# Prompt attention, selected branch: values stationary and exponentials as two float32r parts, the other branch unchanged

## The chip, the cores and the metric

The kernel runs on one core of one Trainium2 chip. The metric is device time in microseconds (us) of one execution, the median of several. In what follows PE is TensorE, PEld its weight loads, DVE VectorE, ACT ScalarE, POOL GpSimd and SP SyncE; SP and ACT also issue transfers.

## What is computed

One inference step of a decoder of two layers, for a prompt of 2048 tokens and eight sample sequences of 8 tokens each. Layer 0 is retention beside sparse attention with three branches (compressed, selected, sliding window); layer 1 is an S5 state-space mixer with a gated output. The change touches the selected branch of the prompt's attention. The reference, cut to it:

```python
s2 = jnp.einsum('bqghd,bgqkd->bqghk', qblk, kg).astype(f32) * scale
p2 = jax.nn.softmax(jnp.where(m2, s2, NEG_INF), axis=-1)
o_sel = jnp.einsum('bqghk,bgqkd->bqghd', p2.astype(vg.dtype), vg)
...
o = gblk[..., 0:1] * o_cmp + gblk[..., 1:2] * o_sel + gblk[..., 2:3] * o_win
```

For each query and group of four heads, `kg` and `vg` are the keys and values of the 8 selected blocks of 64 tokens. The kernel computes the branch densely: every tile of 128 keys up to the query's own, with a large negative bias on blocks that aren't selected.

## The kernel before

The span has three stages: projections and retention to about 780 us; the attention with its output projection from about 816 to 2112; and the S5 layer (setup, a sweep over the tokens that projects its input, the scan, the outputs, a last sweep) to the end. Instructions are written by Python generators that are woven together, and a list scheduler then settles the order on every engine; what an engine does is thus an order fixed when the kernel is built.

**The attention** works in 32 units: unit u is the query tile t = u mod 16 (128 queries) of head group u // 16 (four heads). `first(u)` loads and splits keys and queries (`keys`, L995, `queries`, L1018) and makes the compressed scores; `second(u)` finds the row maxima (`maxima`, L1126: score matmuls L1140 into PSUM, reductions L1142 or, under a mask, L1146 on DVE), writes their negative, times constants, as four extra rows of the queries (L1161 on POOL), and sums the compressed values (`values1`, L1092 to L1102). `body(u)` runs `loop(u, 1)`, the window, then `loop(u, 0)`, the selected branch. While unit u runs its loops, `second(u + 1)`, `first(u + 2)` and a filling stream are woven in: in the first head group the sample sequences, in the second the output projection (`project`, L1299: transposes L224, matmuls L269 to L271 in three float32r parts, additions L1313).

**A loop** takes one step for each key tile k: t + 1 steps in the selected branch (272 over all units), min(t, 4) + 1 in the window (140). A step (L1164 to L1194) makes the scores of 128 keys by 4x128 queries in one PSUM tile `st` (two buffers; matmuls L1186 and L1187 with float32r operands, 512 columns each, and L1189 under a mask), takes the exponential on ACT into `pe` in SBUF (L1191, five buffers), and AVL = 2 steps later multiplies it with the values. This product (`product`, L1173 to L1175) holds the exponentials of one head, 128 keys by 128 queries, as weights and moves the 65 columns of `VP`: 64 values and a column of ones, so that the row sum comes out beside the output. The four heads have a matmul each, into one tile `ot` of PSUM (two buffers):

```python
for h in range(4):
    nc.tensor.matmul(out=ot[:, h], lhsT=pe[:, 128 * h:128 * h + 128], rhs=VP[br][:, k % nt[br]], ...)
```

All four are in float32. At the end of a loop `weighted` (L1203) is put into the list `late`, and `finish` (L1213) behind the selected one; they are written out some steps into a following loop. `weighted` takes the reciprocal of the 65th column (L1207), multiplies it with the gate (L1208), scales the output with it (L1210), all on DVE, and adds it to `o2` on POOL (L1211). `finish` multiplies by the other gate (L1217) and stores the unit's output.

**Behind the attention** come on SP the weights of the odd layer (L188, `wraw`), the sample's tiles and the S5 sweep (L1608 to L1670: normalisation on POOL or DVE, L210 and L1614; transposes L1626; matmuls L1665 to L1667). Before the sweep, or beside it, stands the setup of the S5 parameters (`discretise`: loads L1467 to L1471, a long chain of small DVE operations L1452 to L1580, round trips through memory `at_s`, L1561 to L1563) and what is computed from it in `tables_in` (L1384 to L1424).

## Time and profile before

| | |
|---|---|
| median of 3 runs | 3415.76 us (3409.8 to 3424.2) |
| the profiled execution | 3436.16 us, its span 3434.4 us |
| mean granted clock of TensorE | 0.951 of full speed |
| PE busy | 3190.7 us (93%) |
| PEld busy | 2652.5 us (77%) |
| DVE busy | 1621.4 us (47%) |
| ACT busy | 1077.6 us (31%) |
| POOL busy | 647.5 us (19%) |
| transfers | 362.83 MB, 106 GB/s over the span |

The span reaches from the first to the last instruction on the chip; the execution's own time is 1.8 us longer. Busy shares are means over the whole span; the stages have different limits, so the rows below are taken by stage. A matmul's busy time is taken from its start to its modelled end and overlaps with the next one's; what a matmul adds to the time is read from the chain, where the pieces follow one another.

### The profile page before, as it was taken

The page shows a single profiled execution, that of the slowest core. Times are in us where ns is not written, and L with a number is a line of the kernel's source. Part 1 is how long each engine was busy: PE and PEld are TensorE (multiplying, and loading weights), DVE is VectorE, ACT ScalarE, POOL GpSimd, SP SyncE. Part 2 cuts the span into 40 slices and gives each one's busy share as a digit, 9 for nine tenths or more (in the row PEclk, how much of TensorE's full clock was granted, in tenths as well). Part 3 has the DMA queues.
Part 4 walks back from the last instruction along what each step waited for, and adds up shares of the span by engine and source line. Part 5 has one row for each costly group of instructions (what it writes and reads, how often), then busy time and mean ns, then how long its engine had stood idle before and what let it go on. Part 6 is the DMA issues. An engine that isn't in the chain of part 4 may idle for free.

```text
span 3434.4 us, 47838 instructions
## 1 busy us (share of the span) xinstructions
PE 3190.7 (93%) x17745; PEld 2652.5 (77%) x17745; DVE 1621.4 (47%) x4172; ACT 1077.6 (31%) x2394; POOL 647.5 (19%) x739
## 2 busy tenths in 40 slices
PE   7999999996999999988999998799898497999999
PEld 5888878875778888867888887698676376888887
DVE  6545544444566654446555552547529603111322
ACT  4223312113444443333333332343335233111100
POOL 1211221122211111011111100232439350000000
PEclk9999999997999998878999999799999798999999
DMA  5333531204222222223211112556774286222342
GB/s 171 109 109 136 181 77 38 46 18 129 87 90 81 70 76 70 70 61 100 75 58 54 47 41 80 147 171 184 210 217 136 94 255 179 74 72 72 119 133 89
DMA packets 313680, 362.83 MB, mean 106 GB/s; under 512 B 132296, under 2 KB 225672, under 8 KB 311144
## 3 DMA queue, kind: packets, MB, share of 16 engines
q1 hardware_dynamic: 243576, 240.77, 23.9%
q10 hardware_dynamic: 63632, 73.84, 6.3%
q0 software_dynamic: 6240, 45.17, 3.7%
q8 instruction: 140, 2.29, 0.3%
q14 instruction: 92, 0.75, 0.1%
HBM read 240.50 MB, written 123.31 MB: 106 GB/s over the span
## 4 chain that ended last, share of the span: by engine, by line
PE 70%; DVE 8%; DMA 4%; ACT 1%; issue 1%; SPq 1%; POOL 1%; ACTq 0%; DVEq 0%; POOLq 0%
PE ot L1175 11%; PE mm L269 7%; PE mm L270 7%; PE mm L271 7%; PE tp L1140 4%; PE st L1186 3%; PE st L1187 3%; PE acc L269 2%; PE acc L753 2%; PE acc L271 2%; PE acc L270 2%; PE mm L1667 2%; PE mm L1665 2%; PE mm L1666 2%; DVE scan L1792 1%; PE acc L910 1%
## 5 line engine op out<-in xcount | busy, mean ns | idle before, releaser
L1175 PEld LDWEIGHTS ot<-VP,pe 128*128 128x128 f32 x3296 | 439.2, 198 | 33.1 <-issue 5.6
L1175 PE MATMUL ot<-VP,pe 128*128 128x65 f32 x3296 | 427.9, 275 | 0.0
L1191 ACT ACTIVATE pe<-st 128x512 f32<-128x512 f32 x412 | 243.6, 597 | 374.1 <-PE st L1187 293.3
L269 PE MATMUL mm<-we_hi,hT_hi 128*128 128x512 f32 x768 | 305.3, 398 | 0.2 <-ACT hT_hi L225 0.2
L270 PE MATMUL mm<-we_lo,hT_hi 128*128 128x512 f32 x768 | 303.3, 395 | 0.0
L271 PE MATMUL mm<-we_hi,hT_lo 128*128 128x512 f32 x768 | 302.4, 394 | 0.0
L269 PE MATMUL mm<-wz_hi,hT_hi 128*128 128x512 f32 x384 | 159.0, 414 | 57.8 <-ACT zr L1700 43.6
L1146 DVE CUSTOM_DVE_ANT_0 tp<-tp,tri 128x256 f32<-128x256 f32 (+3 forms) x352 | 173.7, 504 | 78.2 <-PE tp L1140 71.9
L269 PE MATMUL mm<-we,hT_hi 128*128 128x512 f32 x512 | 202.1, 395 | 6.5 <-ACT hT_hi L239 6.2
L270 PE MATMUL mm<-we,hT_hi 128*128 128x512 f32 x512 | 200.4, 391 | 0.0
L271 PE MATMUL mm<-we,hT_lo 128*128 128x512 f32 x512 | 200.3, 392 | 0.0
L1140 PE MATMUL tp<-KA,QA 96*128 96x512 f32 (+6 forms) x576 | 198.5, 394 | 0.7 <-DVE mc L1142 0.3
L1186 PE MATMUL st<-QB,KB 128*128 128x512 f32 x412 | 183.8, 448 | 2.2 <-ACT pe L1191 2.1
L1142 DVE TENSOR_REDUCE mc<-tp 128x1 f32<-128x512 f32 (+2 forms) x196 | 129.7, 671 | 93.7 <-PE tp L1140 92.8
L1187 PE MATMUL st<-QA,KA 100*128 100x512 f32 (+1 forms) x412 | 171.2, 417 | 1.1 <-POOL QA L1161 1.1
L269 PEld LDWEIGHTS mm<-we_hi,hT_hi 128*128 128x128 f32 x768 | 145.0, 189 | 30.6 <-issue 1.0
L271 PEld LDWEIGHTS mm<-we_hi,hT_lo 128*128 128x128 f32 x768 | 144.8, 189 | 30.5 <-issue 0.7
L270 PEld LDWEIGHTS mm<-we_lo,hT_hi 128*128 128x128 f32 x768 | 145.0, 189 | 29.1 <-issue 0.7
L271 PE MATMUL mm<-wz_hi,hT_lo 128*128 128x512 f32 x384 | 155.5, 405 | 5.5 <-POOL hT_lo L240 5.4
L270 PE MATMUL mm<-wz_lo,hT_hi 128*128 128x512 f32 x384 | 155.1, 404 | 0.0
L1665 PE MATMUL mm<-h_hi,wu_hi 128*128 128x256 f32 x512 | 148.9, 292 | 3.3 <-ACT uT_out L1670 3.3
L1161 POOL TENSOR_TENSOR QA<-pms,c_nd 4x512 fp32r<-4x512 f32 x64 | 66.9, 1046 | 439.0 <-ACT pms L1160 421.7
(550 smaller groups left out, 6980.9 us busy)
## 6 DMA issues: line engine op xcount, KB each, us to landing
xT_in<-xT_s SPq DMA_DIRECT2D x48, 512.0 KB
x_in<-x_prompt SPq DMA_DIRECT2D x32, 512.0 KB
xT_s<-xT ACTq DMA_DIRECT2D x32, 512.0 KB
x_in<-x_s SPq DMA_DIRECT2D x32, 512.0 KB
wraw<-w_in_even SPq DMA_DIRECT2D x24, 512.0 KB
qd<-q_s SPq DMA_DIRECT2D x64, 128.0 KB
o_in<-o_s SPq DMA_DIRECT2D x16, 512.0 KB
x_s<-x_in ACTq DMA_DIRECT2D x16, 512.0 KB
```

Of the source, the lines that this page charges most:

```text
L269: nc.tensor.matmul(out=ps[:, 0:n], lhsT=hi[:, k], rhs=whi[:, k], start=k == 0, stop=False)
L270: nc.tensor.matmul(out=ps[:, 0:n], lhsT=hi[:, k], rhs=wlo[:, k], start=False, stop=False)
L271: nc.tensor.matmul(out=ps[:, 0:n], lhsT=lo[:, k], rhs=whi[:, k], start=False, stop=k == 7)
L753: nc.tensor.matmul(out=pp[:, 0:256], lhsT=q["wc"][:, c, lp].rearrange("p r e -> p (r e)"), rhs=xt[:, j].rearrange("p g n -> p (g n)"), sta ...
L1140: nc.tensor.matmul(out=pv[:, h], lhsT=qa[0:kmask, h0 + h], rhs=KA[br][0:kmask, (k0 % nt[br]) * 128:(k0 % nt[br] + w) * 128], start=True, s ...
L1142: nc.vector.tensor_reduce(out=mc[:, h0:h0 + hw, i], in_=pv, axis=AX.X, op=OP.max)
L1146: nc.vector.tensor_tensor_reduce(out=pv[:, h], in0=pv[:, h], in1=tri[:, m0:m0 + w].rearrange("p a b -> p (a b)"), scale=1.0, scalar=-3e38, ...
L1175: nc.tensor.matmul(out=ot[:, h], lhsT=pe[:, 128 * h:128 * h + 128], rhs=VP[br][:, k % nt[br]], start=k == lo and h == 0, stop=k == u and h ...
L1186: nc.tensor.matmul(out=ps, lhsT=KB[br][:, kc], rhs=qb, start=True, stop=False)
L1187: nc.tensor.matmul(out=ps, lhsT=KA[br][0:r0 + 4, kc], rhs=qa[0:r0 + 4].rearrange("p h q -> p (h q)"), start=False, stop=k not in masked)
L1191: nc.scalar.activation(out=pe, in_=ps, func=AF.Exp, scale=0.125)
L1665: nc.tensor.matmul(out=ps[:, 0:256], lhsT=whi[:, k], rhs=hi[:, k], start=k == 0, stop=False)
```

## The change

For the selected branch alone the two operands of the product trade places. The values become the weights: `VP[0]` holds for each key tile 128 columns, 64 of the values rounded to float32r and 64 of what rounding left (hi and lo), made on POOL from a loaded tile `vr` (L1007 and L1008 of the changed kernel). The exponentials become the moving operand, also in two float32r parts: ACT writes the rounded exponential `ph` (L1215) and the full one `pe` (L1216), and DVE subtracts, `pl` = `pe` - `ph` (L1217). The product is two matmuls of 512 columns, `ph` and `pl`, summed in one PSUM tile of 128x512, whose rows are the output's 64 columns from hi and 64 from lo (L1190, L1191). There is no column of ones: POOL sums `pe` over the steps into `ac` (`add`, L1182, none for the first step of a unit). At a unit's end two copies on ACT and an addition on DVE join the halves into `OB`; `total` (in place of `weighted`) transposes the sum (L1244) and the output (L1248) on PE, four matmuls each, reduces the sum on DVE (L1246) and goes on as `weighted` did. The window branch stays as it was. Lines behind L1175 move by up to 52 in the changed kernel (L1142 becomes L1147, L1161 L1166, L1186 L1205, L1313 L1365, L1467 L1519).

```diff
@@ -949,9 +949,11 @@
         KA = [cp.tile([128, nt[i] * 128], F32R, name=f"KA{i}") for i in range(2)]
         KB = [cp.tile([128, nt[i] * 128], F32R, name=f"KB{i}") for i in range(2)]
 
-        VP = [cp.tile([128, nt[i], 65], F32, name=f"VP{i}") for i in range(2)]
-        for v in VP:
-            nc.gpsimd.memset(v[:, :, 64:65], 1.0)
+        VP = [cp.tile([128, nt[0], 2, 64], F32R, name="VP0"), cp.tile([128, nt[1], 65], F32, name="VP1")]
+        T["ac"] = P_("acb", 2)
+
+        OB = T["OB"] = [cp.tile([64, 4, 128], F32, name=f"OB{i}") for i in range(2)]
+        nc.gpsimd.memset(VP[1][:, :, 64:65], 1.0)
         nc.gpsimd.memset(KA[0][96:100].bitcast(F32), 1.0)
         nc.gpsimd.memset(KA[1][64:68].bitcast(F32), 1.0)
 
@@ -1000,7 +1002,10 @@
             for d in range(2):
                 nc.sync.dma_start(out=kd[:, 0, d], in_=self.ks_s[c, 256 + c0:320 + c0])
                 nc.sync.dma_start(out=kd[:, 1, d], in_=self.kw_s[t][:, c0:64 + c0])
-            nc.sync.dma_start(out=VP[0][:, u % nt[0], 0:64], in_=self.ks_s[c, 384 + c0:448 + c0])
+            vr = kv.tile([128, 64], F32, name="vr")
+            nc.sync.dma_start(out=vr, in_=self.ks_s[c, 384 + c0:448 + c0])
+            nc.gpsimd.tensor_copy(out=VP[0][:, u % nt[0], 0], in_=vr)
+            nc.gpsimd.tensor_tensor(out=VP[0][:, u % nt[0], 1], in0=vr, in1=VP[0][:, u % nt[0], 0], op=OP.subtract)
             nc.sync.dma_start(out=VP[1][:, u % nt[1], 0:64], in_=self.kw_s[t][:, 128 + c0:192 + c0])
             nc.sync.dma_start(out=ka[64:96], in_=a["kaux"][:, c])
             ps = tp.tile([128, 4, 128], F32, name="tp")
@@ -1166,11 +1171,25 @@
             lo, masked = span(u, br)
             r0 = 96 if br == 0 else 64
 
-            ot = T["ot"].tile([128, 4, 65], F32, name="ot")
+            ot = T["ot"].tile([128, 4, 65] if br else [128, 512], F32, name="ot", tag="ot")
+            pes, n_add = [], [0]
+
+            def add():
+
+                x, y = pes[0], pes.pop(1)
+                pes[0] = T["ac"].tile([128, 512], F32, name="ac") if n_add[0] == 0 else x
+                n_add[0] += 1
+                nc.gpsimd.tensor_tensor(out=pes[0], in0=x, in1=y, op=OP.add)
+
             qb = c["QB"].rearrange("p h q -> p (h q)")
             prods = []
 
-            def product(k, pe):
+            def product(k, pe, pl):
+                if br == 0:
+                    v = VP[0][:, k % nt[0]].rearrange("p a d -> p (a d)")
+                    nc.tensor.matmul(out=ot, lhsT=v, rhs=pe, start=k == lo, stop=False)
+                    nc.tensor.matmul(out=ot, lhsT=v, rhs=pl, start=False, stop=k == u)
+                    return
                 for h in range(4):
                     nc.tensor.matmul(out=ot[:, h], lhsT=pe[:, 128 * h:128 * h + 128], rhs=VP[br][:, k % nt[br]], start=k == lo and h == 0, stop=k == u and h == 3)
 
@@ -1188,17 +1207,50 @@
                 if k in masked:
                     nc.tensor.matmul(out=ps, lhsT=idr, rhs=triT[:, masked[k]].unsqueeze(1).to_broadcast([128, 4, 128]), start=False, stop=True)
                 pe = T["pp"].tile([128, 512], F32, name="pe")
-                nc.scalar.activation(out=pe, in_=ps, func=AF.Exp, scale=0.125)
-                prods.append((k, pe))
+                if br:
+                    nc.scalar.activation(out=pe, in_=ps, func=AF.Exp, scale=0.125)
+                    prods.append((k, pe, None))
+                else:
+                    ph, pl = [T["pp"].tile([128, 512], F32R, name=n, bufs=3) for n in ("ph", "pl")]
+                    nc.scalar.activation(out=ph, in_=ps, func=AF.Exp, scale=0.125)
+                    nc.scalar.activation(out=pe, in_=ps, func=AF.Exp, scale=0.125)
+                    nc.vector.tensor_tensor(out=pl, in0=pe, in1=ph, op=OP.subtract)
+                    pes.append(pe)
+                    if len(pes) > 1:
+                        add()
+                    prods.append((k, ph, pl))
                 if len(prods) > AVL:
                     product(*prods.pop(0))
                 yield
             for p in prods:
                 product(*p)
-            late.append((n_loop[0], lambda: weighted(u, br, ot)))
-            if br == 0:
+            if br:
+                late.append((n_loop[0], lambda: weighted(u, br, ot)))
+            else:
+                acc, ob = pes[0], T["OB"][u % 2].rearrange("p h q -> p (h q)")
+                nc.scalar.copy(out=ob, in_=ot[0:64])
+                x = TM("ox", 512)[0:64]
+                nc.scalar.copy(out=x, in_=ot[64:128])
+                nc.vector.tensor_tensor(out=ob, in0=ob, in1=x, op=OP.add)
+                late.append((n_loop[0], lambda: total(u, acc)))
                 late.append((n_loop[0], lambda: finish(u)))
             yield
+
+        def total(u, acc):
+
+            c = ctx[u]
+            ps, p = [tp.tile([128, 4, 128], F32, name="tp") for _ in range(2)]
+            for h in range(4):
+                nc.tensor.transpose(ps[:, h], acc[:, 128 * h:128 * h + 128], ident)
+            rs = sm.tile([128, 4], F32, name="rs0")
+            nc.vector.tensor_reduce(out=rs, in_=ps, axis=AX.X, op=OP.add)
+            for h in range(4):
+                nc.tensor.transpose(p[:, h, 0:64], T["OB"][u % 2][:, h], ident[0:64, 0:64])
+            nc.vector.reciprocal(out=rs, in_=rs)
+            nc.vector.tensor_tensor(out=rs, in0=rs, in1=c["gt"][:, :, 1], op=OP.mult)
+            o1 = TM("o1", 4, 64)
+            nc.vector.tensor_tensor(out=o1, in0=p[:, :, 0:64], in1=rs.unsqueeze(2).to_broadcast([128, 4, 64]), op=OP.mult)
+            nc.gpsimd.tensor_tensor(out=c["o2"], in0=c["o2"], in1=o1, op=OP.add)
 
         def weighted(u, br, ot):
 
```

The scheduler's order moves with it, at the places below (of the changed kernel numbers behind a name tell tiles apart).

On PE, in the selected loop of unit 28 (the 13th query tile of the second head group), beside the maxima of unit 29 (`tp`) and the output projection (`acc`), before:

```order
L1186 MATMUL st<-QB,KB_6636 128x512
L1187 MATMUL st<-QA,KA_6634 128x512
L1175 MATMUL ot<-VP_6638,pe 128x65 x4
L1140 MATMUL tp<-KA_6634,QA 128x384
L269 MATMUL acc<-wo_hi,hT_hi 128x512
L270 MATMUL acc<-wo_lo,hT_hi 128x512
L271 MATMUL acc<-wo_hi,hT_lo 128x512
```

and of the change:

```order
L1205 MATMUL st<-QB,KB_6636 128x512
L1206 MATMUL st<-QA,KA_6634 128x512
L271 MATMUL acc<-wo_hi,hT_lo 128x512
L1145 MATMUL tp<-KA_6634,QA 128x512
L1190 MATMUL ot<-ph,VP_6638 128x512
L1191 MATMUL ot<-pl,VP_6638 128x512
L269 MATMUL acc<-wo_hi,hT_hi 128x512
L270 MATMUL acc<-wo_lo,hT_hi 128x512
```

The four products of a step are two, behind the scores of a later step as before, with other matmuls between.

On POOL, around the selected loop of unit 15, the last of the first head group, where the keys and values of the second group are being prepared, before:

```order
L1161 TENSOR_TENSOR QA<-pms,c_nd 4x512
L1056 TENSOR_TENSOR e_13583<-e_13583,s_13666 128x4x16
L1016 CAST KA_6634<-kx 32x128 x3
L1161 TENSOR_TENSOR QA<-pms,c_nd 4x512
L1016 CAST KA_6634<-kx 32x128 x4
L1211 TENSOR_TENSOR o_13347<-o_13347,o_14022 128x256
```

and of the change:

```order
L1182 TENSOR_TENSOR ac<-ac,pe 128x512
L1008 TENSOR_TENSOR VP_6638<-vr,VP_6638 128x64
L1007 CAST VP_6638<-vr 128x64
L1182 TENSOR_TENSOR ac<-ac,pe 128x512
L1008 TENSOR_TENSOR VP_6638<-vr,VP_6638 128x64
L1021 CAST KA_6634<-kx 32x128
L1182 TENSOR_TENSOR ac<-ac,pe 128x512 x2
L1166 TENSOR_TENSOR QA<-pms,c_nd 4x512
L1182 TENSOR_TENSOR ac<-ac,pe 128x512
```

The additions stand between the casts of keys and values and ahead of the nd product L1166.

On SP, the loads of the S5 parameters, before in the projection stage (each `rope` and `cv_s` beside them belongs to that stage):

```order
L674 DMA cv_s<-cvN 128x128
L324 DMA xT_in<-xT_s_173 128x1024
L1467 DMA lsb<-ssm_log_step 128x64
L1469 DMA lam<-ssm_lambda_re 64x64
L1470 DMA B_19983<-ssm_b_re 128x32x16
L1471 DMA craw<-ssm_c_re 128x8x64
```

and of the change behind the last load of the output projection:

```order
L1356 DMA o_in<-o_s_80 128x1024
L257 DMA x_in<-x_prompt 128x1024
L1660 DMA x_in<-x1n_s 64x1024
L188 DMA wraw<-w_in_odd 128x2x512 x7
L1519 DMA lsb<-ssm_log_step 128x64
L1521 DMA lam<-ssm_lambda_re 64x64
L1522 DMA B_21378<-ssm_b_re 128x32x16
L1523 DMA craw<-ssm_c_re 128x8x64
```

The loads, and with them the setup on PE, DVE and ACT that starts from them, come after the attention and after seven of the weight loads.

## Rows read from the trace of the kernel before

**Rows 1.** The page, the chain that ended last: by engine, by line.

```profile
PE 70%; DVE 8%; DMA 4%; ACT 1%; issue 1%; SPq 1%; POOL 1%; ACTq 0%; DVEq 0%; POOLq 0%
PE ot L1175 11%; PE mm L269 7%; PE mm L270 7%; PE mm L271 7%; PE tp L1140 4%; PE st L1186 3%; PE st L1187 3%; PE acc L269 2%; PE acc L753 2%; PE acc L271 2%; PE acc L270 2%; PE mm L1667 2%; PE mm L1665 2%; PE mm L1666 2%; DVE scan L1792 1%; PE acc L910 1%
```

**Rows 2.** Windows: length, busy time and instructions by engine, granted PE clock, DMA share, GB/s.

```profile
1516.00:1600.00 84.00, 60.63 (x310) 50.05 (x310) 45.83 (x139) 29.36 (x76) 14.98 (x22) 0.74 0.31 91
1600.00:2112.00 512.00, 511.85 (x3307) 456.26 (x3305) 259.21 (x795) 186.55 (x410) 57.37 (x71) 1.00 0.17 55
816.00:2112.00 1296.00, 1264.63 (x7869) 1066.17 (x7867) 690.27 (x2339) 519.08 (x1190) 176.01 (x238) 0.95 0.22 69
```

**Rows 3.** The costliest groups: count | busy us, mean ns of one | idle before.

```profile
L1191 ACT ACTIVATE pe<-st 128x512 f32<-128x512 f32 x412 | 243.6, 597 | 374.1 <-PE st L1187 293.3
```

**Rows 4.** Chain of waits, 1900 to 1960 us (unit 28): start us, us, what.

```profile
1921.38 0.44 PE tp L1092 x4
...
1943.49 0.24 PE st L1187
1943.72 0.84 PE ot L1175 x8
```

**Rows 5.** Windows of the 32 selected loops, 16 of each head group, with their sums.

```profile
1345.00:1383.90 38.90, 38.85 (x242) 30.87 (x240) 25.18 (x81) 15.45 (x37) 3.99 (x5) 1.00 0.05 15
...
sum 470.00, PE 466.81 PEld 377.23 DVE 252.04 ACT 186.59 POOL 70.70; mean PE 29.18 PEld 23.58 DVE 15.75 ACT 11.66 POOL 4.42
...
1939.80:1973.20 33.40, 33.40 (x217) 29.84 (x216) 18.95 (x48) 11.57 (x27) 3.74 (x5) 1.00 0.14 51
...
2080.80:2109.40 28.60, 28.60 (x183) 25.50 (x182) 1.37 (x2) 9.55 (x16) 0.36 (x1) 1.00 0.05 19
sum 406.90, PE 386.57 PEld 340.95 DVE 207.11 ACT 144.32 POOL 48.44; mean PE 24.16 PEld 21.31 DVE 12.94 ACT 9.02 POOL 3.03
```

**Rows 6.** DVE subtracts of line 199: duration ns min/median/max, first and last start.

```profile
L199 DVE TENSOR_TENSOR wo_lo<-wraw,wo_hi x16: 673/682/774, 1538.4 to 1558.1; 128x512 fp32r<-128x512 f32 x16
```

**Rows 7.** POOL subtracts of line 240, the same view.

```profile
L240 POOL TENSOR_TENSOR hT_lo<-xT_in,hT_hi x64: 1259/1386/1785, 2430.5 to 2820.5; 128x512 fp32r<-128x512 f32 x64
```

**Rows 8.** Timelines of DVE and POOL in the scan stage: start us, us, what.

```profile
2558.82 1.67 DVE L1789 TENSOR_TENSOR scan<-X,AT 128x512 f32<-128x512 f32 x1
...
2559.90 1.74 POOL L1702 TENSOR_TENSOR zr<-th,zr 128x512 f32<-128x512 f32 x1
```

**Rows 9.** Timelines of DVE and POOL in the attention.

```profile
1939.19 0.87 DVE L1208 TENSOR_TENSOR rs<-rs,gt 128x4 f32<-128x4 f32 x1
...
1940.44 1.95 DVE L1142 TENSOR_REDUCE mc<-tp 128x2 f32<-128x512 f32 x3
...
1939.01 1.03 POOL L1161 TENSOR_TENSOR QA<-pms,c_nd 4x512 fp32r<-4x512 f32 x1 [3.85 <-ACT pms L1160]
1940.65 0.74 POOL L1211 TENSOR_TENSOR o<-o,o 128x256 f32<-128x256 f32 x1 [0.61 <-POOL QA L1161]
```

**Rows 10.** Chain of waits, 2110 to 2210 us; the window before the sweep; line 1395.

```profile
2110.40 1.73 PE ot L1175 x16
...
2171.39 0.60 DVE h_lo L1630
...
2177.11 5.36 DMA at_s<-AT
...
2195.80 2.87 POOL x_in L1614
2198.71 1.97 PE tp L1626 x8
...
2160.00:2198.00 38.00, 18.27 (x96) 15.28 (x96) 22.44 (x72) 9.87 (x20) 4.01 (x4) 0.63 0.46 126
...
L1395 PE MATMUL pq<-c_ident,ab x128: 270/272/331, 2283.8 to 2458.5; 128*128 128x128 f32 x128
```

**Rows 11.** Waits: engine, line, waited for, total us, times, longest.

```profile
POOL KA L1016 <- DMA kx<-kaux: 55.0, 16, 15.7
```

## The prediction

> **What bounds the kernel now.** I read the chain of waits first. TensorE (PE) is on it for 70% of the span, and the selected and window products (L1175) are its largest single line with 11% [rows 1]. Then the windows: from 816 to 2112 us, the attention, PE is busy 1264.63 of 1296 us, and from 1600 on 511.85 of 512 at a granted clock of 1.00 [rows 2]. So there a microsecond of PE work is a microsecond of time, until another engine becomes later. Next, the 32 selected loops, each window reaching from its first score matmul to its last product: 470.00 + 406.90 = 877 us, in which PE is busy 853, VectorE (DVE) 459, ScalarE (ACT) 331 and GpSimd (POOL) 119 us [rows 5]. DVE has the least room of the others, so the forecast turns on what is put there.
>
> **What PE saves.** Unit u's selected loop has (u mod 16)+1 steps, 272 in all. A step's product is four matmuls with 65 moving columns; with their weight loads they take 0.84 us on the chain [rows 4]. The two that take their place move 512 float32r columns through a stationary 128x128, as a score matmul of the same step does: 0.24 us each [rows 4]. So 0.84 - 0.48 = 0.36 us a step; 272 x 0.36 = **-98 us**. No row shows float32r with hi and lo values side by side as weights; I take the scores' price, since type and shape are the same.
>
> **What PE pays.** Each unit now ends with eight transposes, four of the summed exponentials and four of the output. Four take 0.44 us on the chain [rows 4], so 0.88 x 32 = **+28 us**, all of it on a full PE.
>
> **What DVE pays.** Each step adds a subtract of two 128x512 SBUF operands. Alone, such a subtract takes 0.68 us [rows 6], 272 x 0.68 = 185 us. But it doesn't run alone: POOL gets a 128x512 addition for each step but a unit's first (240), at 1.26 us when nothing is beside it [rows 7], and subtract and addition become ready together, when the second exponential is written. In the scan stage, where both engines run such two-operand work, one DVE operation took 1.67 us and the POOL one begun beside it 1.74 [rows 8]. In the attention itself a DVE multiply of 128x4 took 0.87 us, and ended 0.02 us after the POOL instruction that had begun before it, while the reductions, whose operand is in PSUM, kept their 0.65 us beside POOL [rows 9]. I read this as one of the two waiting for the other's whole instruction when DVE reads two SBUF operands. The Trainium skill says so too (GPSIMD Engine Reference, 1. Specifications): GpSimd shares its SBUF interfaces with VectorE, with contention when a DVE instruction has two SBUF inputs. By that rule the attention's loops give back a good part of PE's saving; without it they would keep nearly all.
>
> So the price lies between 0.69 us (DVE always first) and 1.65 (always behind POOL, as in the scan). I take the middle, 1.17, because here POOL isn't always busy: one addition of 1.26 us comes per step of about 3 us. A loop then lasts as long as the longer of two: its duration less 0.36 a step, or its DVE busy time plus the price a step. The loop of 33.40 us at 1939.80 (13 steps): PE 33.40 - 4.68 = 28.7, DVE 18.95 + 15.2 = 34.2, so +0.8. That at 1345.00 (14 steps): 33.9 against 41.6, so +2.7. The last, at 2080.80 (16 steps): 22.8 against 20.1, so -5.8 [rows 5]. Done for all 32, the loops change by -97 us at a price of 0.69, -69 at 1.0, **-40 at 1.17**, +5 at 1.4 and +62 at 1.65. Against -98 the forecast's term for DVE is thus **+58 us**. The operations at a unit's end (an addition, a reduction of 0.65 us [rows 9], a multiply for the one removed) fall into the next unit's window loop: outside the selected loops DVE is busy 690 - 459 = 231 of 419 us [rows 2, 5], so they cost nothing while that cover stands.
>
> **What ACT and POOL pay.** The second exponential costs ACT 272 x 0.597 us [rows 3] = 162 us: 331 + 162 = 493 of some 780 us of loops, hidden. POOL goes from 119 by 240 x 1.26 = 302 to 421 us, hidden as a sum. Its order is another matter: the cast and subtract that split each unit's values stand between the additions, and so does the nd product (L1161), on whose result the next loop's scores wait; I put that at nothing and keep it as a rival. In the last unit no other work remains: 15 additions at 1.26 to 1.74 us are 19 to 26 us against 22.8 on PE, and behind the last product come two copies, an addition, eight transposes and a reduction where three short operations stood. **+9 us** for both.
>
> **What moves behind the attention.** The S5 parameter loads leave their early place on SP and stand behind seven weight loads of the odd layer; the setup computed from them goes later on PE and DVE. Now this setup precedes the S5 sweep: PE is busy 18.27 of the 38 us up to 2198, a round trip through memory holds the chain for 5.36 us, and POOL normalises the sweep's first prompt tile only at 2195.80 [rows 10]. The sample's tile, ahead of it, is through DVE at 2171.39, so with the setup out of the way the sweep could begin near 2172, a gain of up to 25 us; PE first transposes what the setup yields at 2283.8 (L1395) [rows 10], 85 us into the sweep, and in the changed order that stands equally far into it. Against that, late loads can hold up DVE and PE in their order: four such waits would be some 20 us. Between -25 and +20 I take **-10**, nearer the gain, since only one chain is hidden under a full PE.
>
> **The sum.** -98 + 58 + 28 + 9 - 10 = -13 us. The profiled execution took 3436.16 us with a span of 3434.4, 20 us (0.6%) over the median of 3415.76; I apply the difference to the median: 3415.76 - 13 = **3403 us**. About 0.5% (17 us) is what a measurement of this kernel can tell from no change.
>
> **The rivals.** (A) PE stays the bound, because DVE's subtract comes first nearly always, at 0.69 to 1.0 us: loops -97 to -69, so 3415.76 - 97 + 28 + 9 - 10 = 3347 to 3375. For it: POOL is idle most of the time now, and the exponentials have three buffers for each part, so DVE may work ahead. Against: both are released by the same event. Chance 0.27.
>
> (C) The other side: **the subtract waits for POOL's addition each time.** The place is L1217 of the changed kernel against L1182; the price is 1.65 us a step instead of 0.69, the loops become +62 us and the total 3415.76 + 62 + 28 + 9 - 10 = 3505. It decides from about 1.25 us a subtract, where the loops' -27 just pays for the rest. For it: rows 8, which show the full wait on both engines in turn. DVE would then also keep PE waiting, and in the attention's one stretch with an idle PE, 1516 to 1600, the granted clock is 0.74 instead of 1.00 [rows 2], which would add to it. Against: in the scan neither engine had other work, while here POOL has 421 of 780 us. Chance 0.22.
>
> (D) POOL's order: a cast that waits for late values or keys (POOL waits for the key-bias load 16 times, up to 15.7 us [rows 11]) now holds the additions behind it, and with them the nd product that releases the next scores; with it the moved setup stalls the sweep. Two waits of 10 us in the loops and +20 in place of -10: 3403 + 50 = 3453. For it: POOL's queue had slack for such waits, and loses it. Against: the additions have nothing waiting for them within a unit. Chance 0.13.
>
> (E) The change doesn't do what it says, if the two matmuls run at the four's 0.84 us: then PE saves nothing and 28 us come on top, 3444. The scores' 0.24 speaks against it. Chance 0.03.
>
> **How the numbers follow.** The forecast (B), DVE and PE about level, has 0.35, and by itself spans 3380 to 3425. Faster by over 0.5% is below 3399: nearly all of A (0.26) and two fifths of B (0.13), 0.39. Slower is above 3433: C without its lower end, D and E, and a rest of B, 0.36. Same is what remains, 0.25. The range reaches from A's end, 3347, up into C: 3490 leaves the far half of C (0.11) outside, and below 3347 I leave 0.06.
>
> **What would show it.** Right: the product lines at about 0.24 us a matmul on the chain; the subtract at a mean near 1.2 us, with a minimum near 0.69; POOL's addition between 1.26 and 1.74; PE below 97% busy in the loops, waiting for `ph` or `pl`; the transposes of the sum at 0.44 for four; the sweep beginning some 20 us sooner after the last product than the 2198.71 - 2112.13 = 87 us of before [rows 10]. A mean subtract under 0.8 us would make A right, one over 1.4 C. The forecast is wrong in kind if PE waits chiefly for ACT or for POOL's QA, or if the granted clock in the attention falls under its 0.95 [rows 2] and that costs more than the counted work.

## The result and the profile after

The changed kernel is slower: 3455.57 us (median of 4, 3452.8 to 3456.41) beside 3412.78 (4 runs), a ratio of 1.0123 [1.0094, 1.0151], some +43 us. Its profiled execution has a span of 3453.3 us, at the median; that of before lies 23 us above the median of its four runs, so stages are compared as far as they differ by more than that.

The page's busy times, the chain by engine, and the two groups that the change adds to DVE and POOL:

```profile
PE 3157.4 (91%) x16369; PEld 2528.1 (73%) x16369; DVE 1949.5 (56%) x4508; ACT 1241.3 (36%) x2730; POOL 1028.4 (30%) x1042
...
PE 56%; DVE 17%; DMA 4%; ACT 4%; issue 3%; POOL 2%; SPq 0%; ACTq 0%; DVEq 0%; POOLq 0%
...
L1182 POOL TENSOR_TENSOR ac<-ac,pe 128x512 f32<-128x512 f32 x210 | 306.8, 1461 | 107.1 <-ACT pe L1216 91.1
...
L1217 DVE TENSOR_TENSOR pl<-pe,ph 128x512 fp32r<-128x512 f32 x272 | 264.3, 976 | 25.4 <-ACT pe L1216 21.3
```

DVE is on the chain for 17% of the span, where it had 8% [rows 1], and PE for 56 instead of 70. The subtract takes 0.976 us in the mean, between its 0.69 alone [rows 6] and the 1.17 that I took; the addition takes 1.46.

The attention, from its first to its last exponential, in two windows, one for each head group (length, PE, PEld, DVE, ACT, POOL busy, granted clock, DMA share, GB/s):

```profile
800.20:1508.30 708.10, 661.00 (x3512) 484.79 (x3512) 528.78 (x1549) 380.37 (x863) 301.32 (x319) 0.93 0.23 73
1508.30:2143.10 634.80, 573.36 (x2965) 459.79 (x2965) 479.18 (x1122) 300.37 (x660) 252.21 (x217) 0.93 0.19 60
```

Before, the same two windows were

```profile
816.10:1506.60 690.50, 683.36 (x4209) 553.46 (x4208) 379.79 (x1386) 298.27 (x693) 102.62 (x144) 0.93 0.24 76
1506.60:2109.40 602.80, 578.57 (x3637) 510.00 (x3637) 309.19 (x952) 219.74 (x495) 73.39 (x94) 0.96 0.20 62
```

So the second group lost 32 us. The first lost 18, less than the 23; beside before with late loads (below), whose profile lies 5 us under its median, the two groups lost 38 and 34 us. PE has 672 matmul instructions fewer in the second, yet is busy as long (573 us against 579), at a granted clock of 0.93 instead of 0.96, and it idles 61 us instead of 24. PE's largest wait in the attention is one that I had named as a sign, for the subtract's result (total us, times, longest):

```profile
PE ot L1191 <- DVE pl L1217: 39.9, 40, 3.1
```

In the selected loop of unit 28, the one at 1939.80 in [rows 5], from its first exponential to the first of the next loop, 33.4 us before and 36.2 now, DVE is busy 34.0 us:

```profile
1974.90:2011.10 36.20, 31.68 (x140) 23.26 (x139) 34.04 (x58) 19.13 (x41) 20.74 (x16) 0.95 0.13 45
```

The chain of waits through this loop, by line, and two of its pieces (start us, us, what), is now for more than half DVE's work:

```profile
by line: DVE pl L1217 27.8%; issue 13.8%; DVE mc L1147 11.7%; DVE tp L1151 7.1%; PE ot L1191 4.8%; DVE scr L1076 3.3%; PE acc L271 2.9%; PE acc L269 2.6%; PE acc L270 2.6%; PE tp L1105 2.3%; DVE rs L1260 2.1%; DVE im L1069 2.1%; PE st L1206
...
1976.23 0.83 DVE pl L1217
...
1978.25 1.35 DVE pl L1217
```

And the timelines of DVE and POOL at the second of them:

```profile
1978.18 1.42 DVE L1217 TENSOR_TENSOR pl<-pe,ph 128x512 fp32r<-128x512 f32 x1
...
1977.77 1.29 POOL L1182 TENSOR_TENSOR ac<-pe 128x512 f32<-128x512 f32 x1 [1.26 <-ACT pe L1216]
```

The addition runs from 1977.77 to 1979.06; the subtract that started inside it ends at 1979.60, 0.54 us after it: it waited for POOL's instruction, as in [rows 8]. The trace shows how often. Of the 272 subtracts, 131 start inside an addition; 99 of these take over 0.8 us, and each of the 99 ends 0.55 to 0.56 us after the end of its addition. The median subtract, 0.693 us, isn't lengthened; the higher mean comes from this third.

### The profile page after: what moved, and what is told of

It is laid out like the page before. It is cut to its first block, busy times and chain, and to the rows that moved or that the text cites. A ratio compares the mean times of both kernels' runs of the same rounds, so it can differ in the third digit from the quotient of the medians.

```text
span 3453.3 us, 46415 instructions
## 1 busy us (share of the span) xinstructions
PE 3157.4 (91%) x16369; PEld 2528.1 (73%) x16369; DVE 1949.5 (56%) x4508; ACT 1241.3 (36%) x2730; POOL 1028.4 (30%) x1042
## 4 chain that ended last, share of the span: by engine, by line
PE 56%; DVE 17%; DMA 4%; ACT 4%; issue 3%; POOL 2%; SPq 0%; ACTq 0%; DVEq 0%; POOLq 0%
PE mm L269 7%; PE mm L270 7%; PE mm L271 7%; PE ot L1194 4%; DVE pl L1217 4%; PE tp L1145 2%; PE st L1205 2%; PE st L1206 2%; DVE scan L1844 1%; DVE mc L1147 1%; PE acc L910 1%; DVE X L1846 1%; PE acc L269 1%; PE mm L1719 1%; PE acc L753 1%
## 5 line engine op out<-in xcount | busy, mean ns | idle before, releaser
L1182 POOL TENSOR_TENSOR ac<-ac,pe 128x512 f32<-128x512 f32 x210 | 306.8, 1461 | 107.1 <-ACT pe L1216 91.1
L1217 DVE TENSOR_TENSOR pl<-pe,ph 128x512 fp32r<-128x512 f32 x272 | 264.3, 976 | 25.4 <-ACT pe L1216 21.3
L1215 ACT ACTIVATE ph<-st 128x512 fp32r<-128x512 f32 x272 | 162.6, 598 | 186.8 <-PE st L1206 147.4
L1205 PE MATMUL st<-QB,KB 128*128 128x512 f32 x412 | 184.8, 449 | 5.7 <-ACT pe L1211 3.9
L1991 DVE SCALAR_TENSOR_TENSOR th<-th,mm 128x512 f32<-128x512 f32 x32 | 22.0, 687 | 255.5 <-PE mm L271 255.5
L1216 ACT ACTIVATE pe<-st 128x512 f32<-128x512 f32 x272 | 161.4, 594 | 2.3 <-DVE x_in L1365 2.3
L1194 PEld LDWEIGHTS ot<-VP,pe 128*128 128x128 f32 x1120 | 153.0, 202 | 9.5 <-issue 1.6
L1191 PE MATMUL ot<-pl,VP 128*128 128x512 f32 x272 | 120.0, 441 | 40.5 <-DVE pl L1217 39.9
```

The source lines that it names most:

```text
L1182: nc.gpsimd.tensor_tensor(out=pes[0], in0=x, in1=y, op=OP.add)
L1205: nc.tensor.matmul(out=ps, lhsT=KB[br][:, kc], rhs=qb, start=True, stop=False)
L1215: nc.scalar.activation(out=ph, in_=ps, func=AF.Exp, scale=0.125)
L1216: nc.scalar.activation(out=pe, in_=ps, func=AF.Exp, scale=0.125)
L1217: nc.vector.tensor_tensor(out=pl, in0=pe, in1=ph, op=OP.subtract)
```

## The experiments

Four theories. **L**: while an addition on POOL reads SBUF, DVE's operations on SBUF operands wait. **Q**: DVE's queue is too full, whatever the subtract's length. **P**: PE's own added work and its clock. **R**: POOL's queue delays what stands behind the additions. Ratios are to the kernel before, run on the same chip (its medians there 3412.57 to 3414.33). A plain table first, with the attention's two windows as above; kernels without a star have the changed kernel's matmuls. Each kernel is put in order anew when it is built, and PE's order in the attention isn't quite the changed kernel's in any of them, so a part of any difference can be due to that.

| kernel | time, us | ratio | group 1, us | group 2, us | DVE busy, both |
|---|---|---|---|---|---|
| before* | 3413 | 1 | 690.5 | 602.8 | 689 |
| before, late loads* | 3393.61 | 0.9936 | 670.5 | 600.9 | 689 |
| changed | 3455.57 | 1.0123 | 708.1 | 634.8 | 1008 |
| no additions | 3324.6 | 0.9737 | 639.1 | 564.5 | 883 |
| no subtracts | 3384.97 | 0.9908 | 679.1 | 581.2 | 790 |
| neither | 3344.99 | 0.979 | 629.9 | 561.7 | 720 |
| additions of 8 columns | 3332.71 | 0.9757 | 661.7 | 561.9 | 883 |
| additions of 256 columns | 3355.6 | 0.983 | 658.4 | 587.1 | 925 |
| memsets on POOL | 3361.26 | 0.9829 | 682.1 | 566.1 | 890 |
| subtract from PSUM | 3418.64 | 1.0003 | 717.6 | 594.0 | 928 |
| additions on DVE | 3368.4 | 0.9882 | 675.4 | 582.1 | 1014 |
| products four steps behind | 3465.22 | 1.0165 | 717.3 | 631.7 | 1013 |
| sums from a column of ones* | 3338.78 | 0.9797 | 642.6 | 576.8 | 846 |
| the same, both branches* | 3327.27 | 0.9748 | 634.3 | 577.8 | 931 |

**Without the additions.**

```diff
-                    if len(pes) > 1:
-                        add()
...
-                acc, ob = pes[0], ...
+                acc, ob = pes[-1], ...
...
-            nc.vector.reciprocal(out=rs, in_=rs)
+            nc.vector.tensor_scalar(out=rs, in0=rs, scalar1=1.0, scalar2=None, op0=OP.max)
```

(A maximum of the same shape stands for the reciprocal, since the sum of one tile can be zero.)

> The changed kernel without POOL's 240 additions of the exponentials (the row sum is taken from the last key tile alone, so it isn't the softmax's). Theory L (the additions on POOL lengthen DVE's subtracts, and that is what costs): the subtract's mean falls from 0.98 to about 0.70 us, 272 x 0.28 = 76 us of DVE work go, and most of it shows: 3455 falls to 3385 to 3405 us. Theory Q (DVE's queue is too full whatever the subtract's length; PE waits for pl because the subtract stands in a queue with the maxima): the mean falls too, but the time falls by 20 us or less, to 3435 or more. Theory P (PE's own added work and lower clock): no change, 3450 to 3460.

Ratio 0.9737 [0.9698, 0.9776], some 131 us under the changed kernel: more than the 50 to 70 us that L had expected. The subtract is near its length alone, 0.707 us in the mean (its group), and both windows shrink:

```profile
L1217 DVE TENSOR_TENSOR pl<-pe,ph 128x512 fp32r<-128x512 f32 x272 | 191.6, 707 | 35.4 <-ACT pe L1216 30.6 <-PE acc L271 2.1 <-PE ot L1191 0.3
```

```profile
808.10:1447.20 639.10, 619.70 (x3513) 460.11 (x3513) 472.16 (x1548) 377.39 (x863) 125.17 (x204) 0.98 0.25 82
1447.20:2011.70 564.50, 538.26 (x2965) 445.96 (x2964) 410.41 (x1123) 299.29 (x661) 77.14 (x94) 0.97 0.21 67
```

With the same matmuls as the changed kernel, PE is busy 35 us less in the second window (clock 0.97) and idles 26 us instead of 61; DVE is busy 69 us less. P falls. Q, which expected 3435 us or more, falls as well: all 272 subtracts are there, and PE is busy 538 of 564.5 us. (The run with the additions on DVE, below, tests Q at the changed kernel's DVE time.)

**Without the subtracts.**

```diff
-                    nc.vector.tensor_tensor(out=pl, in0=pe, in1=ph, op=OP.subtract)
...
-                    prods.append((k, ph, pl))
+                    prods.append((k, ph, ph))
```

(Both matmuls then move `ph`, so the output isn't the attention's.)

> The changed kernel without the 272 subtracts on DVE (both matmuls move the rounded part ph, so the second part is wrong in its data and PE's work is the same). Theories L and Q both expect most of PE's counted saving back: 264 us of DVE work go, PE waits for pl no more, 3455 falls to 3350 to 3385 us. Theory P: 3430 or more, since PE does the same work.

0.9908 [0.9873, 0.9944], about 70 us under the changed kernel, at the upper end of the expectation. But it is 60 us above the run without additions.

**Without both.** The two edits together.

> The changed kernel without the subtracts and without the additions (both left out as in the two runs before). It shows what PE's work alone makes of the time: by the sum on PE, 98 - 28 = 70 us under before and some 20 to 30 from the moved loads, 3315 to 3350 us. If it comes within 10 us of the run without subtracts alone, the additions cost only through the subtracts (L); if it is over 30 us below that run, they cost something of their own. Theory P: above 3400.

0.979 [0.9752, 0.9829]. In the attention the four corners are 1343 us (both), 1260 (additions alone), 1204 (subtracts alone) and 1192 (neither). So subtracts alone cost 12 us, additions alone 69, and together they cost 71 more than the two: 272 x (0.976 - 0.707) = 73 us, as much, is what the subtract is lengthened by. The additions' own 69 I hadn't foreseen: beside them alone PE idles 67 us instead of 38, at a clock of 0.94 instead of 0.97; what it waits for wasn't followed. In whole times this run lies above that without additions; its stage behind the attention is 28 us longer (2008.3 to 3344.6 us, against 2011.7 to 3319.5), and PE waits 22 us there for a tile of the sweep that POOL normalises (L1663), where the run without additions waits 2.8.

**The moved loads alone.** In the kernel before, an unused tile:

```diff
+        nc.gpsimd.memset(cp.tile([128, 5632], F32, name="room")[:, 0:1], 0.0)
```

> The kernel before with an unused tile of 22 KB per partition among the attention's constants, so that the S5 parameter loads stand behind the attention on SP as in the changed kernel, and nothing else is edited. If the moved loads are worth what the two traces suggest (the attention starts 16 us sooner, the time from the last product to the end of the sweep is 16 us shorter), it is 20 to 32 us faster than before: 3381 to 3393. If the move is worth my term of 10 us, about 3403. If it is worth nothing, 3413, and then the attention lost only some 40 us, not 75.

0.9936 [0.9908, 0.9965], 12 to 31 us faster: the loads' new place (the first of them is issued at 2115.6 us instead of 645.3), which an attention that takes more of SBUF brings with it, is a gain. From the last product to the sweep's first prompt tile on PE it is 64 us here (2085.81 to 2150.27) and 69 in the changed kernel, against 87 before [rows 10]:

```profile
2084.07 1.74 PE ot L1176 x16
...
2147.36 2.86 POOL x_in L1615
2150.27 1.10 PE tp L1627 x8
```

**Additions of 8 columns**, in place in POOL's queue.

```diff
...
-                nc.gpsimd.tensor_tensor(out=pes[0], in0=x, in1=y, op=OP.add)
+                nc.gpsimd.tensor_tensor(out=n_add[1][:, 0:8], in0=x[:, 0:8], in1=y[:, 0:8], op=OP.add)
```

> The changed kernel with POOL's 240 additions at their places in the queue, but over 8 columns instead of 512 (the row sum is again taken from the last key tile alone). Theory L (while an addition runs, DVE's operations on SBUF operands wait): the cost goes with the additions' duration, so with some 0.1 to 0.3 us each the time is that without additions, 3325 to 3345 us, and the subtract's mean 0.70 to 0.75. Theory R (POOL's queue: the waits of the additions for the exponentials hold up the nd product, the casts and the final addition behind them): the waits stay, so 3400 us or more.

0.9757 [0.9722, 0.9793]: no different from no additions in the second window (561.9 us against 564.5), 23 us more in the first.

**Additions of 256 columns**, the same edit with 256.

> As the run with additions over 8 columns, with 256 columns. An addition of 256 columns takes about 0.73 us alone, against 1.26 for 512 and 0.2 to 0.3 for 8. Theory L: the cost grows with the additions' duration, between the 8 us at 8 columns and the 131 us at 512: 50 to 75 us over the run without additions, 3370 to 3400, and the subtract's mean 0.78 to 0.86. If the cost sets in only when DVE has no room left (a threshold): under 3350.

0.983 [0.9809, 0.9851], 31 us over the run without additions, less than the 50 to 75 expected. The second window shows a steady growth, 564.5 without additions, 587.1 at 256 columns, 634.8 at 512, with DVE busy 410, 433 and 479 us, but less than in proportion at the half:

```profile
1462.00:2049.10 587.10, 549.64 (x2965) 448.13 (x2964) 433.36 (x1123) 299.76 (x660) 184.79 (x215) 0.96 0.21 65
```

**POOL as busy, without reading SBUF.**

```diff
-                nc.gpsimd.tensor_tensor(out=pes[0], in0=x, in1=y, op=OP.add)
+                for _ in range(2):
+                    nc.gpsimd.memset(pes[-2], 0.0)
```

> POOL as busy, but without reading SBUF: each addition is replaced by two memsets of 128x512 over an exponential tile that the subtract has done with (the row sum is taken from the last key tile alone). Theory L in the form that POOL's reading of SBUF keeps DVE's two-operand work waiting: the subtract's mean stays at 0.70 to 0.75 us and the time near that without additions, 3325 to 3345 us. If any POOL work on SBUF locks DVE out, the subtract is lengthened as by the additions, 3400 us or more. Theory R (POOL's busy queue itself delays the nd product and the final additions): also 3400 or more, but with a subtract of 0.70.

0.9829 [0.9791, 0.9867], between the two. The windows part it. Two memsets of 0.53 us stand where an addition stood, and the subtract is at its length alone: 99 of the 272 start inside a memset, and none of these takes over 0.694 us. The second group takes 566.1 us, with POOL busy 207.8 (252.2 in the changed kernel):

```profile
L1180 POOL MEMSET pe<- 128x512 f32 x480 | 250.3, 530 | 249.1 <-DVE pl L1215 205.2 <-PE st L1204 11.5 <-DVE mx L789 3.7
...
L1215 DVE TENSOR_TENSOR pl<-pe,ph 128x512 fp32r<-128x512 f32 x272 | 189.8, 700 | 38.9 <-ACT pe L1214 33.9 <-PE acc L271 2.8 <-PE ot L1189 0.2
```

```profile
812.30:1494.40 682.10, 657.07 (x3515) 488.46 (x3513) 479.19 (x1548) 378.64 (x863) 243.40 (x426) 0.92 0.24 76
1494.40:2060.50 566.10, 537.79 (x2964) 445.26 (x2962) 411.27 (x1123) 299.55 (x661) 207.77 (x350) 0.97 0.22 67
```

In the second group a POOL that only writes costs nothing (566.1 against 564.5), where the additions, which read, cost 70: L. The Trainium skill (SBUF — State Buffer, Who interferes with whom) has the same distinction: a DVE instruction with two SBUF inputs contends with a GpSimd instruction that reads SBUF, not with one that only writes it. In the first group, where the sample sequences have work on POOL too, the memsets cost 43 us of the 69 that the additions cost, with a subtract that isn't lengthened. But it isn't POOL's queue that shows there: PE idles 25.0 us against 19.4 without additions, none of its waits there is for a tile of POOL, and the other 37 us are busy time of PE at a granted clock of 0.92 instead of 0.98. That clock isn't tied to the additions alone. In the first group of before it was 0.93, and with late loads, at the same idle time of 7 us, 0.96:

```profile
811.70:1482.20 670.50, 663.31 (x4209) 537.86 (x4209) 378.95 (x1385) 298.24 (x694) 102.29 (x144) 0.96 0.24 78
```

The four times of the kernel with memsets spread from 3339.99 us, at a mean clock of 0.964, to 3364.21 at 0.955, the profiled one. So R isn't shown, and what lowers the clock in the first group stays open.

**The subtract from PSUM.**

```diff
...
-                    nc.scalar.activation(out=pe, in_=ps, func=AF.Exp, scale=0.125)
-                    nc.vector.tensor_tensor(out=pl, in0=pe, in1=ph, op=OP.subtract)
-                    pes.append(pe)
+                    nc.scalar.activation(out=ps, in_=ps, func=AF.Exp, scale=0.125)
+                    nc.vector.tensor_tensor(out=pl, in0=ps, in1=ph, op=OP.subtract)
+                    pes.append(ph.bitcast(F32))
```

> The changed kernel with the full exponential written back into its PSUM tile, so that the subtract has one operand in PSUM and one in SBUF; POOL adds the rounded parts (the row sum is that of the rounded exponentials). Theory L: the subtract no longer waits for the additions, mean 0.65 to 0.72 us, 70 us of DVE work go; the other DVE operations are still lengthened as in the run without subtracts, so 3385 to 3410 us. If the score tile, now held until the subtract, is what ends last, PE waits for st and it comes to 3430 or more. Theory R: 3440 to 3460, since POOL's queue is the same.

1.0003 [0.998, 1.0027], 3418.64 us: between the 3385 to 3410 and the 3430 or more of the expectation. Beside 240 additions (1.30 us in the mean), none of its subtracts takes more than 0.694 us, though 163 start inside an addition:

```profile
L1217 DVE TENSOR_TENSOR pl<-st,ph x272: 652/682/694, 819.5 to 2118.9; 128x512 fp32r<-128x512 f32 x136
...
L1182 POOL TENSOR_TENSOR ac<-ac,ph x210: 1262/1288/1613, 877.2 to 2118.5; 128x512 f32<-128x512 f32 x105
```

So one operand in PSUM frees it. The second window falls to 594.0; the first doesn't (717.6, at a clock of 0.90). PE now waits 18 us for score tiles that the subtract holds, and 15 us instead of 40 for `pl`; why the clock is so low in the first group stays open.

**The additions on DVE.**

```diff
-                nc.gpsimd.tensor_tensor(out=pes[0], in0=x, in1=y, op=OP.add)
+                nc.vector.tensor_tensor(out=pes[0], in0=x, in1=y, op=OP.add)
```

> The changed kernel with the 240 additions on DVE instead of POOL. Theory L: POOL locks nothing any more, subtract and addition take 0.70 us each; DVE gets 240 x 0.70 = 168 us more than in the run without additions and comes level with PE in the loops, so 3350 to 3400 us, clearly under 3455 although DVE does more work. Theory Q (DVE's queue is too full): as slow as the changed kernel or slower, 3450 or more.

0.9882 [0.9851, 0.9914], 87 us under the changed kernel with DVE as busy as there:

```profile
1480.70:2062.80 582.10, 550.90 (x2965) 444.41 (x2965) 473.43 (x1240) 298.99 (x660) 77.59 (x93) 0.96 0.20 64
```

473 us of DVE in 582, against 479 in 635. So DVE's total isn't what costs; the same time costs more when it comes as waits that the fixed order doesn't foresee. That this is the difference is argued from these two rows; no run shows it by itself.

**The products four steps behind.** In the selected loop, with five buffers of `ph` and `pl` and four of `pe`.

```diff
-                if len(prods) > AVL:
+                if len(prods) > (AVL if br else 4):
```

> The changed kernel with the products four steps behind the scores in the selected loop, not two, and five buffers for each part of the exponentials. If PE waits for pl only because each comes a little late (latency), the deeper queue takes most of the 40 us of PE's waits and some of the clock's loss: 3380 to 3420 us. If DVE can't keep up over a whole loop (throughput, with the lock), the wait only moves to later steps: 3435 to 3460 us.

1.0165 [1.0131, 1.0199]: no gain from a longer queue. PE's wait for `pl` falls by half, and its waits for other tiles of DVE grow; that for L777's, 14.8 us here, is 4.0 in the changed kernel:

```profile
PE ot L1191 <- DVE pl L1217: 21.3, 18, 3.2
...
PE tp L781 <- DVE cvT L777: 14.8, 5, 4.2
```

So the wait moves, as the second case of the expectation has it, though 3465 is above its 3460.

**Sums from a column of ones.** As the additions cost so much, a version without them. `VP[0]` now has 65 columns for each of its two parts, ones behind hi and zeros behind lo:

```diff
...
+                    v = VP[0][:, k % nt[0]]
+                    nc.tensor.matmul(out=ot, lhsT=v[:, 0], rhs=pe, start=k == lo, stop=False)
+                    nc.tensor.matmul(out=ot, lhsT=v[:, 1], rhs=pe, start=False, stop=False)
+                    nc.tensor.matmul(out=ot, lhsT=v[:, 0], rhs=pl, start=False, stop=k == u)
```

> A version without additions: three matmuls a step, hi with a column of ones by ph, lo with a column of zeros by ph, hi with ones by pl, so that the row sum comes out of PE; at a unit's end one copy and four transposes. PE: 3 x 0.24 = 0.72 us a step in place of 0.48, 272 x 0.24 = +65 us against the run without additions, and -14 for four transposes fewer: 3325 + 51 = 3376 us, 3365 to 3385, if PE is the bound and nothing on DVE waits for POOL. Under R or P nothing else is expected of it. Against before that would be some 38 us faster, of which 20 are the moved loads.

0.9797 [0.9766, 0.9827]: faster than before and than the change, by more than I had counted. The chain in its loop of unit 28, and in that of before with late loads:

```profile
1925.84 0.23 PE ot L1191
1926.07 0.23 PE ot L1192
1926.29 0.23 PE ot L1193
1926.52 0.23 PE acc L269
```

```profile
1925.81 0.84 PE ot L1176 x8
1926.65 0.29 PE acc L269
1926.93 0.23 PE acc L270
```

Three matmuls take 0.69 us where I counted 0.72, and the old product's 0.84 makes the piece behind it 0.29 instead of 0.23. So a step saves 0.21 us, not 0.12. The additions and the copy that fall away at a unit's end come on top.

**The same for both branches.** Against the version before:

```diff
...
-                if br:
-                    nc.scalar.activation(out=pe, in_=ps, func=AF.Exp, scale=0.125)
-                    prods.append((k, pe, None))
...
-                    v = VP[0][:, k % nt[0]]
+                v = VP[br][:, k % nt[br]]
```

> The version with ones as a 65th column for both branches, the window too: 140 more steps of three float32r matmuls in place of four float32 ones, which in the run with ones gained about 0.19 us a step on PE, 27 us, less 32 x 0.24 = 8 for four transposes a unit: 3339 - 19 = 3320 us. DVE gets 140 x 0.69 = 97 us more and ACT 84 more, in window loops where DVE is busy some 270 of 460 us; if that is too much there, no gain or a loss, 3335 to 3360.

0.9748 [0.9723, 0.9774], 3327.27 us: the lowest median of the versions that compute all of it, though its interval overlaps with that of the ones in the selected branch alone.

## Why the prediction was wrong

The forecast was 3403 us with DVE and PE about level; it came to 3455.57, inside the range, which reached up into rival C, and on the other side. (By its own sum rival A would reach from 3346 to 3374 us, 1 us below the ends given. And the 32 windows of [rows 5] don't end with a loop's last product, but with the next loop's first exponential: in unit 28 the product ends at 1969.8, the window at 1973.2. The sums over them hold.)

**PE's saving and its transposes** were right. I counted -98 + 28 = -70 us; from before with late loads to the run without additions the time falls by 3393.61 - 3324.6 = 69 us. (The chains just shown make a step's saving 0.90 - 0.46 = 0.44 us rather than 0.36, some 20 us in all; the subtracts' own 12 us hide part of that.) So rival E is out: the new product isn't as dear as the old. Rival A's price, 0.69 to 1.0 us a subtract, was met, and yet PE didn't stay the bound at 3347 to 3375 us; it does so only without the additions, with all 272 subtracts in place.

**The moved loads** were right in kind, -10 for -21 measured, in the range of -25 to +20.

**The price of the subtract** was too high: 0.976 measured for 1.17. By my own formula the loops should then have changed by -73 us. They changed by -9 (from 877 to 868), and the window loops by +59, where I had counted the 28 of the transposes. Without the additions the two are 754 and 450 us. Beside before with late loads (857 and 415) that is -103 and +35, near my -98 and +28; so it is the additions that undo PE's saving.

**The step that failed** is "a loop then lasts as long as the longer of two", with DVE's busy time from before plus the subtract alone. Three things were missing. First, the additions lengthen other DVE operations too, not the subtract alone; the masking of the compressed probabilities (L1062) goes from a median of 0.455 to 0.612 us with the additions, up to 1.765. In the run without additions and in the changed kernel (duration ns min/median/max, first and last start):

```profile
L1062 DVE SCALAR_TENSOR_TENSOR e<-e x32: 192/455/810, 787.3 to 1922.0; 128x32 f32<-128x32 f32 x2, 128x64 f32<-128x64 f32 x2, 128x96 f32<-128x96 f32 x2, 128x128 f32<-128x128 f32 x2
```

```profile
L1062 DVE SCALAR_TENSOR_TENSOR e<-e x32: 193/612/1765, 787.6 to 2045.3; 128x32 f32<-128x32 f32 x2, 128x64 f32<-128x64 f32 x2, 128x96 f32<-128x96 f32 x2, 128x128 f32<-128x128 f32 x2
```

DVE's busy time in the attention is 1008 us against 883 without additions, and 73 of the 125 are the subtract's. Second, PE and DVE wait for each other in turn, so that in unit 28 neither is full (34.0 and 31.7 of 36.2 us); the longer of the two is no bound that the loop reaches. With each loop's measured DVE time in my formula, the 32 loops come to some 815 us; they took 868. Third, the granted clock: with the same matmuls PE was busy 1234 us in the attention at 0.93, where it idled 109 us, and 1158 at 0.98 without additions, where it idled 46. Of the 139 us between the two, 76 are busy time and 63 idle time. By an estimate from the two mean clocks, 1158 x 0.98 / 0.93 = 1220, some 62 of the 76 are the clock's. It shows in the window loops, which took 475 us instead of 450 though DVE is as busy there with the additions as without (284 and 283 us). I had the clock as an addition to rival C and as a sign that the forecast is wrong in kind, and gave it no price. What lowers it isn't shown.

**Rival C** had the side, and its wait for POOL's whole instruction is real, but not "each time": it lengthens 99 of 272 subtracts. Its point, "from about 1.25 us a subtract", came from the failed step: 0.976 was enough. The sign I had named for C, a mean over 1.4, would have misled. The Trainium skill's sentence (GPSIMD Engine Reference, 1. Specifications), that GpSimd's SBUF interfaces are shared and contend with DVE instructions with two SBUF inputs, is borne out: beside the same additions the mean was 0.976 us with both operands in SBUF and no subtract took over 0.694 with one in PSUM. **POOL's order**, which I put at nothing and kept as rival D, isn't shown to cost anything: the 43 us of the memsets are nearly all lower clock. That D's 3453 us is so close to the measured time is luck; the waits of POOL for the key-bias load, my reason for it, were 27 us in all, fewer than the 55 of before [rows 11]. **The last loop** was right: its chain ends in additions on POOL, 1.62 us each, and the loop of unit 31 took 24 us:

```profile
2143.38 1.62 POOL ac L1182
...
2145.07 1.62 POOL ac L1182
```

## What to carry to other kernels

Work that is "hidden" on POOL wasn't free here, where it read SBUF (131 us): price it by every DVE operation on two SBUF operands that it will meet, or see whether that operation can have one operand in PSUM (0.684 us in the mean instead of 0.976 here). Two engines that feed each other within a step, each some nine tenths full as in unit 28, can take longer than the longer of the two: both wait, and here PE's clock was lower on top. When an epilogue needs a sum, look first whether a matmul already there can carry it in a spare column, even at the price of one more matmul.

## What was not expected

Taking room away in SBUF made the kernel before 21 us faster: parameter loads, and the setup that follows them, no longer stand in front of a stage that needs none of it for 85 us. With the additions on DVE the kernel was 87 us faster than with them on POOL, at the same DVE busy time (1014 and 1008 us). And memsets on POOL, 0.53 us each and two for an addition, left the subtract at 0.700 us in the mean.
